# A two-layer decoder trunk: maxima over partitions taken by GpSimd, and a reordered first layer

## The chip, the cores and the metric

The kernel runs on one core of one Trainium2 chip. The metric is the time of one execution on the device in microseconds (us); before the change the median of two runs is 1400.21 us (1398.36 to 1402.06). Engines are named as in the profile: PE (matmul) with PEld (its weight loads), DVE (VectorE), ACT (ScalarE), POOL (GpSimd) and SP (which issues the DMAs here).

## The reference

One sequence of 1024 tokens with 1024 channels in float32 goes through two layers. Each layer projects x to [main | memory query | main gate | memory gate], computes a main branch and a cross-attention into 256 memory tokens (4 heads of 128), gates both with silu, projects back and normalizes:

```python
h = x @ w_in
y_main = main_fn(h[..., :D_MAIN])
y_mem = memory_attention(q_mem, mem, w_mem_kv)
y = concat([y_main * silu(g_main), y_mem * silu(g_mem)])
x = layer_norm(ALPHA * x + y @ w_out, ln_g, ln_b)
```

In layer 0 the main branch is a causal pooling: four groups of 256 channels, trailing means over 2, 4, 8 and 16 tokens minus the token, then a 256x256 map per group and a scale per channel. In layer 1 it is causal attention of 16 heads with forget gates. The change touches layer 0 alone.

## The kernel before, in words

Everything stands transposed: channels on the 128 partitions, tokens along the free axis. A float32 product is made of three products of parts. There are two ways to cut a number.

*Plain parts* (`hi_lo`, lines 168-173): `hi` is the float32r copy (ACT, L171), `lo` the remainder in bf16 (DVE, L172) and `top` a bf16 copy of the number (ACT, L173, or POOL, L166, where a caller passes `gp_copy`). `three` (L162) pairs them: hi with hi, top with lo, lo with top. `split_w` loads a weight piece of 128x512 on SP and cuts it.

*Scaled halves* (`halves_of`, L253-255): a number times a power of two as an f16 value (ACT, L254) and its f16 remainder (DVE, L255). This needs a scale that holds for the whole tensor, so a maximum over all partitions: `bound` (L234-245) reduces on DVE (L238), writes 128 numbers to DRAM (SP, L239), reads all of them back into each partition (SP, L241), reduces again (DVE, L242) and rounds to a power of two (L243, L244). `scale_of` inverts it (L249, L250).

`slab_pair` (L257-321) computes two column slabs of x @ w_in (two times 128 channels by 1024 tokens) in seven steps of 12 products, 84 in all, in place of 96, by Strassen's scheme in Winograd's form. It loads four weight blocks, takes their absolute sums (ACT, L266), calls `bound`, forms four differences of blocks on POOL (L273), and then for each step cuts one block or difference with `halves_of` and multiplies it with one of seven combinations of x (`XC`). The evacuations (L279, L287, L299) undo the scale. The first subtraction writes the tile into which the absolute values of L266 are thrown, so it waits for them.

Layer 0 runs in this order:

1. x is loaded in eight tiles and cut in plain parts (`load_x`, L626-632); two slabs of pooling group 0 are computed plainly (`slab`, L698-702). ACT sums absolute values of x (L706), and `bound` is called for x (L707).
2. Memory keys and values are projected, four heads each (`mem_kv`, L328-369, products of L347). After each head but the first, `combine` (L719-725) cuts one of the seven combinations of x in halves: 28 splits of 128x512 on ACT and DVE. In between POOL forms 16 differences and sums of blocks of x in place (L725).
3. `pooled(0)` forms the pooled values of group 0. Two `slab_pair`s make the four memory queries, cut again in plain parts; one makes the gates of group 0; `pool_out` (L666-681) multiplies the pooled values with their map.
4. Memory attention, with two `slab_pair`s of gates pumped in between.
5. For groups 1, 2, 3: a pair of inputs, `pooled`, a pair of gates, `pool_out`, and some weights of the output projection (`out_proj.split`). Then the output projection.

So `bound` is called twelve times: once for x and once in each of eleven pairs. PE's order is written out by hand (`manual_schedule`); the other engines' orders are planned by the framework from the program's order and when operands come. Each engine runs its instructions in its order, and SP its DMAs: a DMA that waits holds those behind it. Weight blocks land in a ring of six `raw` tiles, the cut ones in a ring of eight `w` tiles.

Of the kernel before, what the change touches and what calls it, by code (L numbers as in the profile page):

```python
# [18 lines left out]
P = 128  # L19
# [53 lines left out]
def trunk_kernel(ctx, tc, x, xT, memT, win, wk, wv0, wv, wmk, wmv, wout, poolw, pscale, lng, lnb, bforget, out):  # L73
# [74 lines left out]
    class Split:  # L148
# [5 lines left out]
        def __getitem__(self, at):  # L154
            part = Split.__new__(Split)
            part.hi, part.lo, part.top = self.hi[at], self.lo[at], self.top[at]
            return part

# [9 lines left out]
    def hi_lo(to, src, pinned=False, top=None):  # L168

        pin = tc.keep_in_program_order if pinned else lambda ins: ins  # L170
        pin(nc.scalar.copy(to.hi, src))  # L171
        pin(nc.vector.tensor_tensor(to.lo, src, to.hi.bitcast(F32), ALU.subtract))  # L172
        (top or nc.scalar.copy)(to.top, src)  # L173
# [6 lines left out]
    def split_w(src_dram, shape):  # L180
        r = raw(shape)
        nc.sync.dma_start(r, src_dram)
        to = parts_of(wt, shape)
        (gp_hi_lo if low[0] else hi_lo)(to, r)
        return to
# [48 lines left out]
    def bound(sums):  # L234

        m, e = tiny(1), tiny(1)
        d = dram.tile([P, 1], F32, name=nm("bound"))
        nc.vector.tensor_reduce(m, sums, AX.X, ALU.max)  # L238
        nc.sync.dma_start(d, m)  # L239
        every = sb([P, P], "every", 2, F32, more[0])  # L240
        nc.sync.dma_start(every, d.rearrange("p o -> (p o)").partition_broadcast(P))  # L241
        nc.vector.tensor_reduce(m, every, AX.X, ALU.max)  # L242
        nc.vector.tensor_scalar(m, m, 2.0 ** -100, None, ALU.max)  # L243
        nc.vector.tensor_scalar(e.bitcast(I32), m.bitcast(I32), 0x7F800000, None, ALU.bitwise_and)  # L244
        return e
# [10 lines left out]

    def slab_pair(one, two, XC, dest, done):  # L257
# [3 lines left out]
        sums = tiny(4)  # L261
        for b, src in zip(bs, (one[0], two[0], two[1], one[1])):
            nc.sync.dma_start(b, src)
        for j, b in enumerate(bs):
            junk = ts[0].rearrange("p a b -> p (a b)").bitcast(BF16)[:, :NH].rearrange("p (a b) -> p a b", a=4)
            nc.scalar.activation(junk, b, AF.Abs, accum_out=sums[:, j : j + 1])  # L266
        e = bound(sums)
        sc = scale_of(e, "wsc")
        un = sb([P, 1], "wun", 3, F32, more[0])
        nc.vector.tensor_tensor(un, e, xun, ALU.mult)  # L270
# [57 lines left out]
    def mem_kv(l):  # L328

        ms = [parts_of(T, [P, 4, NMEM]) for _ in range(2)]  # L330
# [6 lines left out]
        def project(w_dram):  # L337

            acc = ps([P, NH], "pj", 2)[:, :NMEM]
            ws = [split_w(w_dram[pc], [P, 4, P]) for pc in range(2)]  # L340
            parts = (1, 2, 0) if len(projected) % 2 else (0, 1, 2)
            projected.append(acc)
            for i in parts:
                for pc in range(2):
                    w, m = three(ws[pc], ms[pc])[i]
                    for k in range(4):
                        nc.tensor.matmul(  # L347
                            acc, w[:, k, :], m[:, k, :],
                            start=(i, pc, k) == (parts[0], 0, 0), stop=(i, pc, k) == (parts[2], 1, 3),
                        )  # L350
                        if k % 3 == 0:
                            spread()
            return acc
# [259 lines left out]
    X = parts_of(stream, [P, KT, S])  # L613
# [5 lines left out]
    with tc.tile_pool(name="in0", bufs=1) as in0:  # L619
# [6 lines left out]
        def load_x(kt, parts=1):  # L626
            r = bt(dt=F32)
            for i in range(parts):
                cols = slice(i * S // parts, (i + 1) * S // parts)
                nc.sync.dma_start(r[:, cols], xT[kt, :, cols])  # L630
                hi_lo(X[:, kt, cols], r[:, cols], top=gp_copy)
            xs.append(r)

        first = [[split_w(win[0, 0, 0], [P, 4, P])], []]
        load_x(0, 2)
        first[1].append(split_w(win[0, 1, 0], [P, 4, P]))
        for kt in range(1, 4):
            load_x(kt)
        for f in range(2):
            first[f].append(split_w(win[0, f, 1], [P, 4, P]))  # L640
# [76 lines left out]
        changes = {0: ((b21, b21, b22, ALU.add), (b11, b21, b11, ALU.subtract)), 3: ((b21, b22, b11, ALU.subtract),), 2: ((b12, b12, b11, ALU.subtract),)}  # L717

        def combine(k):  # L719
            src = (b11, b11, b12, b21, b21, b12, b22)[k]  # L720
            for kt in range(4):
                halves_of(XC[0][k][:, :, kt, :], src[kt], xsc)
            for to, a, b, op in changes.get(k, ()):
                for kt in range(4):
                    nc.gpsimd.tensor_tensor(to[kt], a[kt], b[kt], op)  # L725

        with tc.manual_schedule(engines={PE}):
            kv = mem_kv(0)
            for h in range(2 * MH):
                kv[1 + h // MH](h % MH)  # L730
                if h:
                    combine(h - 1)
            pms = pooled(0, us)
            qs = [parts_of(bt, [P, S]) for _ in range(MH)]
# [452 lines left out]
```

## Time and profile before

| | us |
|---|---|
| median of two runs | 1400.21 |
| the profiled execution | 1397.46 |
| its span, first to last instruction | 1395.8 |
| PE busy in the span | 1202.3 |
| DVE, ACT, POOL busy | 908.1, 758.4, 337.1 |

The mean granted clock of the tensor engine is 0.932. The profile shows one execution. A page lists busy times, the span in 40 slices, DMA queues and the costliest groups of instructions. Other views give busy time by stretch, waits (who waited for whom, in total, how often, the longest), and a timeline (start, duration, engine, line, operation, output<-input, and in brackets the idle time before it and what ended it). A line can be that of a helper: L172 is every remainder of plain parts.

### The profile page before, as it was taken

To read this page: it belongs to the slowest core of one execution; us is meant where nothing else is said; L and a number is where in the kernel's file an instruction comes from. 1 tells how busy PE (TensorE), PEld (TensorE's weight loads), DVE (VectorE), ACT (ScalarE), POOL (GpSimd) and SP (SyncE) were. 2 spreads that over 40 slices of the span, in tenths; PEclk is the share of its full clock that TensorE was granted. 3 is DMA by queue.
4 is the path that set the end of the run, shared out by engine and by line. 5 is a ranking of instruction groups with operands and counts; after the bars stand their busy time and mean duration, and the time that the engine had idled before them with its cause. 6 is when DMAs were issued, how large, how long until landed. Compare 5 with 4: busy or idle time off the path is not lost. (4 is left out here: it accounts for less than half of the span.)

```text
span 1395.8 us, 20190 instructions
## 1 busy us (share of the span) xinstructions
PE 1202.3 (86%) x6886; PEld 726.7 (52%) x6886; DVE 908.1 (65%) x2033; ACT 758.4 (54%) x1605; POOL 337.1 (24%) x429
## 2 busy tenths in 40 slices
PE   8635857557776689998999999999999999999997
PEld 4422323333332245556667766666666666665554
DVE  7774536566665754557357457888788788876564
ACT  7674425445443462336577336777677677767220
POOL 6431110112332300000000004434443453462000
PEclk9777988788998889999999999999999999999999
DMA  6343332344332262334244447799698698998331
GB/s 199 90 80 54 47 52 56 65 113 85 70 77 55 78 218 76 106 113 145 69 110 112 126 113 166 162 197 189 150 201 198 154 193 191 222 225 261 133 130 61
DMA packets 270871, 179.48 MB, mean 129 GB/s; under 512 B 214192, under 2 KB 229168, under 8 KB 270768
## 3 DMA queue, kind: packets, MB, share of 16 engines
q1 hardware_dynamic: 270768, 178.19, 52.7%
q8 instruction: 54, 0.88, 0.3%
q14 instruction: 49, 0.40, 0.1%
HBM read 95.76 MB, written 22.62 MB: 85 GB/s over the span
## 5 line engine op out<-in xcount | busy, mean ns | idle before, releaser
L223 PE MATMUL pj<-A,w 128*128 128x512 bf16 (+1 forms) x1872 | 448.6, 391 | 5.3 <-ACT A L171 2.4
L314 PE MATMUL pj<-A,w 128*128 128x512 f16 x696 | 172.8, 410 | 87.8 <-ACT w L254 36.2
L223 PEld LDWEIGHTS <-w 128*128 128x128 bf16 x1264 | 114.0, 98 | 140.6 <-issue 19.4
L314 PEld LDWEIGHTS <-w 128*128 128x128 f16 x696 | 72.3, 104 | 184.6 <-issue 78.6
L978 DVE SCALAR_TENSOR_TENSOR P<-T,s,P 128x512 f16<-128x512 f32 x192 | 111.5, 613 | 34.8 <-ACT P L977 33.5
L956 ACT ACTIVATE T<-MK,s 128x512 f32<-128x512 f32 x192 | 111.3, 580 | 41.6 <-DVE s L948 23.4
L223 PEld LDWEIGHTS pj<-A,w 128*128 128x128 f32 x624 | 115.2, 190 | 31.0 <-ACT A L171 4.6
L977 ACT ACTIVATE P<-T,s 128x512 f16<-128x512 f32 x192 | 102.7, 576 | 45.9 <-ACT T L956 20.7
L542 PEld LDWEIGHTS <-T 128*128 128x128 bf16 x736 | 70.9, 98 | 88.5 <-issue 6.4
L200 PE MATMUL L<-B,B 128*128 128x512 f32 (+3 forms) x384 | 106.4, 382 | 2.7 <-DVE s L948 2.5
L314 PE MATMUL pj<-A,wx 128*128 128x512 f16 x228 | 54.3, 394 | 46.4 <-ACT wx L254 43.0
L940 POOL TENSOR_SCALAR_AFFINE_SELECT R<-R 128x128 f32<-128x128 f32 x128 | 41.0, 326 | 175.2 <-DVE s L948 129.1
L200 PEld LDWEIGHTS L<-B,B 128*128 128x128 f32 x384 | 70.6, 189 | 24.1 <-DVE s L948 6.1
L166 POOL TENSOR_SCALAR w<-raw 128x512 fp32r<-128x512 f32 x108 | 67.1, 627 | 65.0 <-PE pj L223 59.7
L948 DVE CUSTOM_DVE_ANT_0 MK<-L,R 128x512 f32<-128x512 f32 (+3 forms) x128 | 72.5, 566 | 9.1 <-PE L L200 3.6
L177 POOL TENSOR_TENSOR w<-raw,w 128x512 bf16<-128x512 f32 x54 | 69.5, 1286 | 18.7 <-PE pj L223 16.2
L347 PE MATMUL pj<-T,w 128*128 128x256 bf16 (+1 forms) x336 | 51.5, 307 | 23.5 <-ACT w L173 6.9
L853 POOL MEMSET G<- 128x128 f32 x1 | 0.2, 205 | 293.4 <-DVE V L484 293.4
L172 DVE TENSOR_TENSOR T<-T,T 128x1024 bf16<-128x1024 f32 x23 | 28.1, 1223 | 58.4 <-ACT T L171 36.4
L172 DVE TENSOR_TENSOR w<-raw,w 128x512 bf16<-128x512 f32 x55 | 42.0, 764 | 32.1 <-PE pj L223 14.8
L314 PEld LDWEIGHTS <-wx 128*128 128x128 f16 x228 | 22.8, 101 | 75.6 <-ACT wx L254 43.8
L1000 PE MATMUL O<-T,V 128*64 128x128 f16 (+1 forms) x1152 | 57.6, 221 | 2.7 <-DMA T<-P 2.6
(323 smaller groups left out, 2290.7 us busy)
## 6 DMA issues: line engine op xcount, KB each, us to landing
raw<-in_win_dram SPq DMA_DIRECT2D x80, 256.0 KB, 2.8
raw<-in_wout_dram SPq DMA_DIRECT2D x33, 256.0 KB, 3.1
B<-B SPq DMA_DIRECT2D x32, 256.0 KB, 4.1
R<-cumd SPq DMA_DIRECT2D x16, 512.0 KB, 4.9
y0d<-Y SPq DMA_DIRECT2D x12, 512.0 KB, 2.7
T<-y0d SPq DMA_DIRECT2D x12, 512.0 KB, 3.6
T<-y1d SPq DMA_DIRECT2D x11, 512.0 KB, 5.2
rawx<-in_win_dram SPq DMA_DIRECT2D x16, 256.0 KB, 2.6
```

The source lines that it names most:

```text
L166: nc.gpsimd.tensor_scalar(to, src, 1.0, 1.0, ALU.mult, ALU.mult)
L172: pin(nc.vector.tensor_tensor(to.lo, src, to.hi.bitcast(F32), ALU.subtract))
L177: nc.gpsimd.tensor_tensor(to.lo, src, to.hi.bitcast(F32), ALU.subtract)
L200: nc.tensor.matmul(acc, a, b, start=i == 0, stop=i == len(terms) - 1)
L223: nc.tensor.matmul(accs[n], a[:, k, :], b[:, pc * 4 + k, n * NH : (n + 1) * NH], start=seen[n] == 1, stop=seen[n] == 3 * KT,)
L314: nc.tensor.matmul(bank[name], w[:, e0, kt, :], xc[:, e1, kt, :], start=bool(opens) and i == kt == 0, stop=k in (2, 5, 6) and i == 2 and k ...
L542: nc.tensor.matmul(accs[a][nh], y, w, start=kt == 8 and i == 0, stop=kt == 7 and i == 2,)
L948: nc.vector.tensor_tensor_reduce(p[:, lo:up], lg, R[:, lo:up], 1.0, top, ALU.add, ALU.min, m[:, n : n + 1])
L956: nc.scalar.activation(e, p[:, lo:up], AF.Exp, bias=top, scale=-1.0, accum_out=sums[:, n, hd % 2, i : i + 1],)
L977: nc.scalar.activation(pair[:, lo:up], e, AF.Copy, scale=r)
L978: nc.vector.scalar_tensor_tensor(pair[:, L + lo : L + up], e, r, pair[:, lo:up], ALU.mult, ALU.subtract)
L1000: nc.tensor.matmul(acc[rows, (i % 4) * P : (i % 4) * P + P], v[:, b, 2 * j : 2 * j + (1 if e else 2), :].rearrange("p e d -> p (e d)"), pt ...
```

## The change

- `bound` no longer goes through DRAM: between DVE's first reduction and the rounding stands one GpSimd instruction, an all-reduce (max) of one number over 128 partitions. Two DMAs, one DVE reduction and a 128x128 tile go.
- A class `Same` has `top` equal to `hi`, and its `lo` is float32r. x, the first four weight pieces of the first two slabs, the memory and its weights in layer 0 are cut so: the third copy goes, and the two smaller products are float32r products.
- The first two memory queries are computed by a new `two_slabs`: the same scaled halves, but four weight blocks with four blocks of x in 96 products, with no differences. It evacuates into plain parts at once.
- `combine` becomes `combos`: four blocks of x are cut first (two beside the value heads 0 and 1, two after the memory), 8 block splits in all in place of 7; POOL's 16 operations on x and the last four splits come after `two_slabs` in the program. `pooled(0)` moves behind the second query pair.
- Groups go in the order 3, 2, 1, and the `pool_out` of a group comes after the next group's pair of inputs.

```diff
     def bound(sums):
-        m, e = tiny(1), tiny(1)
-        d = dram.tile([P, 1], F32, name=nm("bound"))
+        m, every, e = tiny(1), tiny(1), tiny(1)
         nc.vector.tensor_reduce(m, sums, AX.X, ALU.max)
-        nc.sync.dma_start(d, m)
-        every = sb([P, P], "every", 2, F32, more[0])
-        nc.sync.dma_start(every, d.rearrange("p o -> (p o)").partition_broadcast(P))
-        nc.vector.tensor_reduce(m, every, AX.X, ALU.max)
-        nc.vector.tensor_scalar(m, m, 2.0 ** -100, None, ALU.max)
+        nc.gpsimd.partition_all_reduce(every, m, P, bass_isa.ReduceOp.max)
+        nc.vector.tensor_scalar(m, every, 2.0 ** -100, None, ALU.max)
...
+    class Same(Split):
+        def __init__(self, hi, lo):
+            self.hi = self.top = hi
+            self.lo = lo
...
-        (top or nc.scalar.copy)(to.top, src)
+        if not isinstance(to, Same):
+            (top or nc.scalar.copy)(to.top, src)
...
+    def two_slabs(one, two, xh, xun, junk, evac):
+        bs = [[raw([P, 4, P]) for _ in range(2)] for _ in range(2)]
+        for p in range(2):
+            for j, src in enumerate((one, two)):
+                nc.sync.dma_start(bs[p][j], src[p])
+        sc, un = pair_scale(bs[0] + bs[1], junk, xun)
+        ws, accs = {}, {}
+        for half in range(2):
+            for p in range(2):
+                for j in range(2):
+                    if half == 0:
+                        ws[p, j] = wt([P, 2, 4, P], F16)
+                        halves_of(ws[p, j], bs[p][j], sc)
+                    if p == 0:
+                        accs[half, j] = ps([P, NH], *(("pj", 2) if half == 0 else ("L", 3)))
+                    acc = accs[half, j]
+                    for i, (e0, e1) in enumerate(((0, 0), (0, 1), (1, 0))):
+                        for kt in range(4):
+                            nc.tensor.matmul(acc, ws[p, j][:, e0, kt, :], xh[half][p][e1][:, kt, :],
+                                start=p == i == kt == 0, stop=p == 1 and i == 2 and kt == 3)
+                    if p == 1:
+                        evac(j, slice(half * NH, (half + 1) * NH), acc, un)
...
-        ms = [parts_of(T, [P, 4, NMEM]) for _ in range(2)]
+        make = parts_of if l else same_of
+        ms = [make(T, [P, 4, NMEM]) for _ in range(2)]
...
-    X = parts_of(stream, [P, KT, S])
+    X = same_of(stream, [P, KT, S])
...
+        def combos(k):
+            if k == 0:
+                direct(b11, xh[0][0])
+            if k == 1:
+                direct(b12, xh[0][1])
+            if k == 2:
+                direct(b21, extra)
+            if k == 3:
+                direct(b22, xh[1][1])
+            if k == 4:
+                change(b21, b21, b22, ALU.add)
+                change(b11, b21, b11, ALU.subtract)
+                direct(b11, [XC[0][1][:, e] for e in range(2)])
+            if k == 5:
+                direct(b21, [XC[0][3][:, e] for e in range(2)])
+                change(b12, b12, b11, ALU.subtract)
+                change(b21, b22, b11, ALU.subtract)
+            if k == 6:
+                direct(b21, [XC[0][4][:, e] for e in range(2)])
+                direct(b12, [XC[0][5][:, e] for e in range(2)])
...
                 kv[1 + h // MH](h % MH)
-                if h:
-                    combine(h - 1)
-            pms = pooled(0, us)
+                if h in (4, 5):
+                    combos(h - 4)
             qs = [parts_of(bt, [P, S]) for _ in range(MH)]
-            for h in (0, 2):
-                wide = [G() for _ in range(2)]
-                run(plain_pair(8 + h, wide, lambda j, cols, t: hi_lo(qs[h + j][:, cols], wide[j][:, cols])))
+            combos(2)
+            combos(3)
+            two_slabs(win[0, 8], win[0, 9], xh, xun, ..., q_evac)
+            for k in (4, 5, 6):
+                combos(k)
+            wide = [G() for _ in range(2)]
+            run(plain_pair(10, wide, lambda j, cols, t: hi_lo(qs[2 + j][:, cols], wide[j][:, cols])))
+            pms = pooled(0, us)
...
-            for g in range(1, 4):
+            late = None
+            for k, g in enumerate((3, 2, 1)):
                 us = [u_tile() for _ in range(2)]
                 run(plain_pair(2 * g, us))
+                if late:
+                    pool_out(*late)
                 pms = pooled(g, us)
                 ys = [y_tile() for _ in range(2)]
                 run(gate_pair(12 + 2 * g, ys))
-                pool_out(g, pms, ys)
-                out_proj.split((4, 8, 8)[g - 1])
+                late = g, pms, ys
+                out_proj.split((4, 8, 8)[k])
+            pool_out(*late)
```

`direct` cuts a block of x in halves in four splits of 128x512 (ACT and DVE), `change` is four POOL operations of 128x512, and `pair_scale` holds the absolute sums, `bound` and the scale that stood in `slab_pair`.

More of the change, by code (lines that the diff above doesn't have):

```diff
@@ L4 @@
 import concourse.bass as bass
+import concourse.bass_isa as bass_isa
 import concourse.tile as tile
@@ L255, in halves_of, with pair_scale @@
         nc.vector.scalar_tensor_tensor(to[:, 1], src, sc, to[:, 0], ALU.mult, ALU.subtract)
+    def pair_scale(bs, junk, xun):
+        sums = tiny(len(bs))
+        for j, b in enumerate(bs):
+            nc.scalar.activation(junk, b, AF.Abs, accum_out=sums[:, j : j + 1])
+        e = bound(sums)
+        un = sb([P, 1], "wun", 3, F32, more[0])
+        nc.vector.tensor_tensor(un, e, xun, ALU.mult)
+        return scale_of(e, "wsc"), un
+    def two_slabs(one, two, xh, xun, junk, evac):
[16 more added lines that the diff above has]
+                        for kt in range(4):
+                            nc.tensor.matmul(
+                                acc, ws[p, j][:, e0, kt, :], xh[half][p][e1][:, kt, :],
+                                start=p == i == kt == 0, stop=p == 1 and i == 2 and kt == 3,
+                            )
+                    if p == 1:
+                        evac(j, slice(half * NH, (half + 1) * NH), acc, un)
     def slab_pair(one, two, XC, dest, done):
@@ L260, in slab_pair @@
         b11, b12, b22, b21 = bs = [raw([P, 4, P]) for _ in range(4)]
-        sums = tiny(4)
         for b, src in zip(bs, (one[0], two[0], two[1], one[1])):
             nc.sync.dma_start(b, src)
[L264 to L270, printed above, removed]
+        sc, un = pair_scale(
+            bs, ts[0].rearrange("p a b -> p (a b)").bitcast(BF16)[:, :NH].rearrange("p (a b) -> p a b", a=4), xun,
+        )
         t1, t2, t3, t4 = ts
@@ L339, in project @@
             acc = ps([P, NH], "pj", 2)[:, :NMEM]
-            ws = [split_w(w_dram[pc], [P, 4, P]) for pc in range(2)]
+            ws = [split_w(w_dram[pc], [P, 4, P], make) for pc in range(2)]
             parts = (1, 2, 0) if len(projected) % 2 else (0, 1, 2)
@@ L639, in trunk_kernel @@
         for f in range(2):
-            first[f].append(split_w(win[0, f, 1], [P, 4, P]))
+            first[f].append(split_w(win[0, f, 1], [P, 4, P], same_of))
         for kt in range(4, KT):
```

40 lines of the change are left out of this document (26 added, 14 removed).

## The prediction

> **What bounds the kernel now.** I read the page first (engines, slices), then busy time by stage, then the waits of the tensor engine, of VectorE and of the DMA queue SP, then the timeline of one bound.
>
> ```profile
> PE 1202.3 (86%) x6886; PEld 726.7 (52%) x6886; DVE 908.1 (65%) x2033; ACT 758.4 (54%) x1605; POOL 337.1 (24%) x429
> PE   8635857557776689998999999999999999999997
> ```
> ```profile
> 0.00:36.00 36.00, 29.80 (x106) 14.32 (x106) 25.29 (x42) 28.13 (x47) 22.03 (x19) 0.91 0.62 193
> 36.00:91.00 55.00, 34.24 (x192) 24.97 (x192) 45.34 (x76) 37.51 (x71) 23.02 (x15) 0.75 0.31 91
> 91.00:114.00 23.00, 0.34 (x3) 0.13 (x2) 6.55 (x21) 8.31 (x16) 3.78 (x3) 0.57 0.45 48
> 114.00:152.00 38.00, 32.50 (x132) 13.81 (x131) 19.21 (x32) 19.40 (x40) 11.30 (x8) 0.86 0.47 57
> 152.00:192.00 40.00, 33.14 (x147) 15.00 (x144) 20.74 (x34) 14.66 (x24) 1.27 (x1) 0.91 0.11 37
> 192.00:313.00 121.00, 62.72 (x458) 38.86 (x456) 65.40 (x146) 53.04 (x148) 14.66 (x11) 0.77 0.40 77
> 313.00:418.00 105.00, 82.08 (x336) 35.19 (x337) 68.39 (x106) 51.87 (x98) 32.85 (x22) 0.87 0.41 81
> 418.00:502.00 84.00, 58.57 (x242) 25.74 (x241) 58.32 (x88) 38.05 (x65) 21.93 (x17) 0.86 0.26 70
> 502.00:1396.00 894.00, 868.87 (x5282) 558.73 (x5280) 598.89 (x1494) 507.44 (x1103) 206.24 (x334) 0.99 0.62 156
> ```
>
> The columns are the stretch, its length, busy time of PE, PEld, DVE, ACT and POOL, the granted clock, the DMA share and GB/s. From 502 us on PE is busy 869 of 894 us, and the change touches none of that. Layer 0, the first 502 us, holds PE for 333 us: 169 us are idle, at a clock of 0.57 to 0.91. The waits of PE in that part say where:
>
> ```profile
> PE pj L314 <- ACT wx L254: 43.0, 2, 22.5
> PE pj L314 <- ACT w L254: 36.2, 2, 22.7
> PE pj L314 <- DVE e L279: 22.0, 7, 6.0
> PE pj L314 <- DVE s L243: 9.8, 1, 9.8
> PE pj L314 <- ACT P L299: 8.6, 1, 8.6
> PE pj L314 <- DVE s L244: 7.3, 1, 7.3
> PE pj L314 <- ACT G L299: 6.9, 1, 6.9
> PE pj L347 <- DVE s L243: 5.8, 1, 5.8
> PE L L200 <- DVE Y L680: 5.7, 1, 5.7
> ```
> ```profile
> DVE s L242 <- DMA every<-bound: 81.3, 11, 13.4
> ```
> ```profile
> SPq L241 <- DMA bound<-s: 79.8, 12, 7.8
> ```
>
> Each wait is us in total, times, longest. L254 cuts weights with a scale that waits for `bound`; L243, L244, L279, L299 and L680 stand behind L242 on VectorE or wait for the same scale. Twelve times a maximum goes to DRAM and comes back: VectorE is held at L242 for 81.3 us in all, SP at L241 for 79.8 us with the weight loads behind it. One of them in order of time:
>
> ```profile
> 93.25 1.04 ACT L171 CAST T<-G 128x1024 fp32r<-128x1024 f32 x1
> ...
> 95.14 0.63 ACT L266 ACTIVATE A<-raw 128x512 bf16<-128x512 f32 x1
> ...
> 98.42 0.16 DVE L238 TENSOR_REDUCE s<-s 128x1 f32<-128x4 f32 x1 [1.63 <-ACT A L266]
> 98.46 1.26 POOL L273 TENSOR_TENSOR A<-raw,raw 128x512 f32<-128x512 f32 x1 [10.83 <-ACT A L266]
> 98.63 0.56 SPq L239 DMA_DIRECT2D bound<-s  x1
> ...
> 99.80 2.60 POOL L273 TENSOR_TENSOR A<-raw,A 128x512 f32<-128x512 f32 x2
> ...
> 111.92 0.29 DVE L242 TENSOR_REDUCE s<-every 128x1 f32<-128x128 f32 x1 [13.35 <-DMA every<-bound]
> ...
> 113.79 15.27 PE L314 MATMUL pj<-A,w 128*128 128x512 f16 x60 [22.66 <-ACT w L254]
> ```
>
> The round trip is 111.92 - 98.63 = 13.3 us, and the scale adds 1.9 until the first product. The three Pool subtractions that the second product needs (L273) are over long before.
>
> **The change, part by part.** Durations are of the profiled execution, 1397.5 us for a span of 1395.8; the median of the runs, 1400.2, is 2.7 above it, and I add that at the end.
>
> *The bounds.* Two DMA issues and a wait leave SP, one 0.29 us reduction leaves VectorE, twelve reductions over partitions enter GpSimd. VectorE's next instruction (the max with 2^-100) now waits for POOL instead of a DMA; behind it stand the same evacuations, and PE behind those. No row shows that reduction. Below, it is bounded by a POOL copy of one column; above, nothing bounds it but the trip that it replaces is the first mark.
>
> ```profile
> 343.36 0.65 POOL L656 COPY G<-P 128x1 f32<-128x1 f32 x1
> ```
> ```profile
> DMA to landing us min/median/max: 3.3/6.0/9.4
> ```
>
> So 0.65 us at one end and 13.3 or more at the other. I take the nearer kind of row: something that must collect a value from 128 partitions, the outward leg of the old trip, 6.0 us to its landing. In POOL's queue the subtraction of 98.46 starts as VectorE's reduction ends, and the next two follow without a gap, so up to three of 1.3 stand before the new instruction: 6.0 + 3.9 = 9.9 us from sums to maximum, 3.4 less than 13.3. Some of that goes back: the subtractions left behind it now end after the maximum, where they had ended 9 us before it. I take 3.0 a bound. The nine waits of PE above sum to 145 us; without the first pair's 22.7 and the 5.8 of the memory stage, 117 us stand behind the ten other pair bounds, 11.7 each, so 3.0 can come out in full: -30. The bound of x is in the memory stage below. By the bounds: a maximum in 2 us would give about -9 each, one in 20 us +7 each.
>
> [...]
>
> *First slabs and memory as float32r pairs.* Gone are the third part's copies: 9 on POOL (x) and 24 on ACT (4 + 16 weight pieces, 4 memory pieces).
>
> ```profile
> L166 POOL TENSOR_SCALAR A<-B 128x1024 bf16<-128x1024 f32 (+1 forms) x9 | 14.1, 1574 | 5.7 <-DMA B<-in_xT_dram 5.7
> ```
> ```profile
> L255 DVE SCALAR_TENSOR_TENSOR A<-B,xsc,A 128x512 f16<-128x512 f32 x28 | 26.1, 963 | 0.7 <-ACT A L254 0.4
> L725 POOL TENSOR_TENSOR B<-B,B 128x512 f32<-128x512 f32 x12 | 20.9, 1758 | 7.7 <-DVE A L255 7.7
> L254 ACT ACTIVATE A<-B,xsc 128x512 f16<-128x512 f32 x28 | 18.6, 715 | 0.0
> L173 ACT CAST w<-raw 128x512 bf16<-128x512 f32 x11 | 6.8, 620 | 0.0
> L725 POOL TENSOR_TENSOR B<-B 128x512 f32<-128x512 f32 x4 | 6.3, 1594 | 12.5 <-DVE A L255 12.5
> ```
> ```profile
> L223 PE MATMUL pj<-A,w 128*128 128x512 bf16 x415 | 100.0, 381 | 0.0
> L223 PE MATMUL pj<-A,w 128*128 128x512 f32 x202 | 54.6, 404 | 0.0
> ```
>
> That is 14.1 us of POOL and 24 x 0.62 = 14.9 of ACT. On PE 64 slab products turn from bf16 to f32, by the last rows (of 1000 to 1200 us) 23 ns more each: +1.5. In the first 36 us PE is busy 29.8, so little is to be had: -2 after that cost (from +2 to -5).
>
> *Memory stage (36 to 91 us).* PE needs 34.2 of 55; VectorE is busy 45.3, ACT 37.5. Twenty casts leave ACT (12.4). Of the 28 splits of x (26.1 on VectorE, 18.6 on ACT) only 8 stay at the values' heads, 24 follow (one block of x is split twice as often, 32 in all). VectorE falls to about 45.3 - 20 x 0.96 = 26, ACT to 37.5 - 12.4 - 20 x 0.72 = 11, and PE's 34 plus 3 (128 products at 23 ns more) becomes the limit. The 5.8 us behind x's bound shrink too. Floor 37, ceiling 55; I take 43, as the loads and each head's evacuation still break PE's stream: -12.
>
> *First query pair plain.* The casts of the pooled values that kept ACT until 95.14 come later in the program (4 us), and this pair has no subtractions before its reduction (13.3 - 6.0 = 7.3): -11. It has 96 products instead of 84, at 15.27/60 = 0.25 us: +3. The 16 differences of x (20.9 + 6.3 = 27 us of POOL) lay under the memory stage; now they, and 16 splits, must end under these 96 products (24 us), with the second pair's reduction and subtractions in the same queue. I count 27 + 5 + 6 - 24, less the 12 of the 48 products that stand before the first that needs the last of them: +2 of a new wait. Together -6 (from -15 to +12).
>
> *Pooling products a pair later.* One wait of 5.7 us (L200 behind L680) is nearly all a VectorE held by L242, already counted; the pooled values get a pair's time, over 30 us. -2.
>
> Sum: -30 - 2 - 12 - 6 - 2 = -52; 1397.5 - 52 = 1345.5, and with the 2.7 to the median 1348.
>
> **The rivals.** *Cheap reduction:* POOL answers in about 4 us from sums to maximum, as a queue with a 0.65 us copy allows. Then ten bounds and the first give 6 more each: 1348 - 65 = 1283. For it: POOL had been idle for 10.8 us before 98.46, so nothing need stand ahead of the reduction. Against: all 128 partitions must meet.
>
> *Gain given back in POOL:* reduction and subtractions do not follow each other freely, so the maximum comes early but the second product's operand late, and the pair starts as late as before. Then -30 becomes about 0 and the differences of x cost some 4 more: 1382. For it: second products now depend on work behind the reduction. [...]
>
> *Slower:* the reduction holds POOL's queue so long that VectorE waits longer at L243 than at L242 now. All else gives -22, so from 13.3 + 2.2 = 15.5 us on the kernel is slower, and from 18.3 by 2%. At 20 us: 10 x 10.1 more than forecast, 1449. For it: nothing above bounds the price, and three trips of it would stand in line before the second query pair. Against: the trip already pays two landings in DRAM.
>
> **How the numbers follow.** My forecast 0.40 (own range 1325 to 1374), cheap 0.20 (1260 to 1325), given back 0.18 (1370 to 1405), slower 0.22 (1405 to 1490). Faster by over 2% (about what a measurement can tell from no change) is below 1372: 0.38 + 0.20 + 0.02 = 0.60. Slower is above 1428: 0.19 of the last case. The rest, 0.21, is the same. Half of the cheap case lies below 1285 and half of the slow one above 1432: those are the ends.
>
> **What would show it.** Right: the wait of VectorE's max for POOL near 7 to 10 us, 13 before; SP no longer stopped; the memory stage about 43 us; layer 0 over near 450 us. Wrong: a wait above 13 us there (slower); the first product early and the second waiting for L273's successors (given back); the second query pair's second and fifth steps waiting for x's differences longer than 5 us; a memory stage still of 55 us, which would mean that its loads set it.

## The result, and the profile after

The changed kernel takes 1346.27 us (median of two runs, 1342.56 to 1349.98) beside 1400.21: a ratio of 0.9615 with a 95% interval of 0.9488 to 0.9741. A later run of the same two kernels with more executions (e7 below), the one that the experiments are set against, gave 1346.17 beside 1409.43, a ratio of 0.9544 (0.9521 to 0.9568). The forecast was 1348.0 in a range of 1285 to 1432. The profiled execution after takes 1342.56 us for a span of 1340.8; its mean granted clock is 0.955, it was 0.932.

Engines and PE's slices from the page of the changed kernel, then its busy time by stage (the columns are those of the prediction's tables; the bounds stand where each stage's last or first product stands now):

```profile
PE 1195.3 (89%) x6826; PEld 734.4 (55%) x6898; DVE 901.9 (67%) x2017; ACT 746.5 (56%) x1580; POOL 323.0 (24%) x428
PE   8668764876878899989999999999999999999997
```
```profile
0.00:32.50 32.50, 28.65 (x105) 20.19 (x106) 20.52 (x48) 28.01 (x45) 2.12 (x8) 0.95 0.71 257
32.50:71.00 38.50, 27.81 (x193) 26.55 (x192) 37.14 (x55) 25.82 (x53) 19.90 (x13) 0.87 0.29 98
71.00:83.90 12.90, 0.02 (x1) 0.02 (x2) 11.16 (x28) 7.58 (x15) 5.48 (x5) 0.64 0.18 41
83.90:157.60 73.70, 66.46 (x288) 29.16 (x289) 40.06 (x66) 34.15 (x59) 15.35 (x13) 0.95 0.16 51
157.60:270.10 112.50, 66.70 (x459) 39.90 (x458) 65.19 (x144) 53.52 (x148) 12.86 (x12) 0.81 0.29 82
270.10:445.60 175.50, 141.63 (x573) 59.73 (x577) 128.55 (x187) 89.95 (x161) 61.19 (x45) 0.92 0.25 82
445.60:1341.00 895.40, 864.09 (x5215) 558.82 (x5281) 599.29 (x1494) 507.45 (x1103) 206.09 (x334) 0.99 0.62 155
```

Set against the lengths of the same stages before (the prediction's rows, with 38 and 40 taken together, and 105 and 84):

| stage | before | after | difference |
|---|---|---|---|
| first slabs | 36.0 | 32.5 | -3.5 |
| memory | 55.0 | 38.5 | -16.5 |
| wait for the first query product | 23.0 | 12.9 | -10.1 |
| queries, gates of group 0, its pooling products | 78.0 | 73.7 | -4.3 |
| memory attention with two pairs of gates | 121.0 | 112.5 | -8.5 |
| groups | 189.0 | 175.5 | -13.5 |
| the rest | 894.0 | 895.4 | +1.4 |

All of the gain is in layer 0, which ends at 445.6 us in place of 502. The waits of PE, VectorE and SP in the first 450 us of the changed kernel (total, times, longest, in us):

```profile
PE pj L352 <- ACT w L261: 61.4, 10, 17.1
PE pj L293 <- ACT w L261: 12.9, 1, 12.9
PE pj L352 <- DVE e L317: 10.9, 6, 4.0
PE pj L352 <- DVE w L262: 9.9, 6, 2.9
PE pj L386 <- ACT MK L184: 7.8, 3, 4.7
```
```profile
DVE s L250 <- POOL s L249: 21.0, 9, 8.2
```
```profile
SPq L305 <- DVE w L262: 90.1, 19, 13.3
```

In the changed kernel's numbering L249 is the all-reduce and L250 the max behind it, L311 the subtractions of a pair, L352 a pair's products, L293 those of `two_slabs`, L261 and L262 the halves of weights, L317 an evacuation, L386 the memory's products, L763 and L767 the splits and differences of x. VectorE's stop at the bound fell from 81.3 us to 21.0, and SP's at it is gone: what SP waits longest for now is a weight tile that VectorE has yet to read. But PE still waits 61.4 us for scaled weights (L261), so the bound is cheaper and not cheap. One bound in order of time, on VectorE, POOL and PE (start, duration, instruction, in brackets the idle time before it):

```profile
166.51 0.16 DVE L248 TENSOR_REDUCE s<-s 128x1 f32<-128x4 f32 x1 [1.64 <-ACT A L268]
166.56 1.26 POOL L311 TENSOR_TENSOR A<-raw,raw 128x512 f32<-128x512 f32 x1 [26.38 <-ACT A L268]
...
174.45 0.38 POOL L249 PARTITION_ALL_REDUCE s<-s  x1 [6.63 <-issue]
174.86 0.15 DVE L250 TENSOR_SCALAR s<-s 128x1 f32<-128x1 f32 x1 [8.19 <-POOL s L249]
...
176.47 1.89 PE L352 MATMUL pj<-A,w 128*128 128x512 f16 x4 [17.15 <-ACT w L261]
```

From the sums (166.51) to the maximum (174.86) it takes 8.35 us; over the eleven bounds of weights it is 4.8 to 10.7 us, where it had been 12.0 to 13.5 before. The reduction itself is 0.38 us of that. One subtraction, 1.26 us, slips ahead of it, and then POOL stands for 6.63 us with "issue" as the reason: it waits for nothing that the profile shows. POOL's own timeline shows the same pause on the way back:

```profile
166.56 1.26 POOL L311 TENSOR_TENSOR A<-raw,raw 128x512 f32<-128x512 f32 x1 [26.38 <-ACT A L268]
174.45 0.38 POOL L249 PARTITION_ALL_REDUCE s<-s  x1 [6.63 <-issue]
181.54 1.25 POOL L311 TENSOR_TENSOR A<-raw,A 128x512 f32<-128x512 f32 x1 [6.71 <-issue]
182.87 1.27 POOL L311 TENSOR_TENSOR A<-rawx,A 128x512 f32<-128x512 f32 x1
```

So POOL loses 6.63 us here when it goes from a subtraction to a reduction and 6.71 on the way back, and 0.08 between two subtractions. The view of line L249 shows what marks these places:

```profile
L249 POOLq MODIFY_POOL_CONFIG  x24: 3/11/13, 1.6 to 403.4; - x24
L249 POOL PARTITION_ALL_REDUCE s<-s x12: 376/377/385, 24.2 to 409.9; - x12
```

An instruction of POOL's sequencer, MODIFY_POOL_CONFIG, of some 11 ns, carries the reductions' line 24 times. The subtractions' line (L311) has 22 more, of 82 to 83 ns, and that of x's differences (L767) two of 83, and always two stand together: 24 changes from one kind of work to the other, twelve into a reduction and twelve out of it. In POOL's timeline a pause of 5.7 to 7.2 us stands at each, but for the first, which falls into a longer idle time. So each return to the other kind of work pays again. What POOL does in the pause, the trace does not show.

### The profile page after: what moved, and what is told of

The parts are those of the page before. It is cut to its first block, busy times and chain, and to the rows that moved or that the text cites. A ratio compares the mean times of both kernels' runs of the same rounds, so it can differ in the third digit from the quotient of the medians.

```text
span 1340.8 us, 20096 instructions
## 1 busy us (share of the span) xinstructions
PE 1195.3 (89%) x6826; PEld 734.4 (55%) x6898; DVE 901.9 (67%) x2017; ACT 746.5 (56%) x1580; POOL 323.0 (24%) x428
## 3 DMA queue, kind: packets, MB, share of 16 engines
HBM read 94.97 MB, written 22.61 MB: 88 GB/s over the span
## 5 line engine op out<-in xcount | busy, mean ns | idle before, releaser
L234 PE MATMUL pj<-A,w 128*128 128x512 bf16 (+1 forms) x1827 | 441.7, 390 | 7.6 <-ACT A L181 2.2
L352 PE MATMUL pj<-A,w 128*128 128x512 f16 x624 | 159.0, 414 | 78.5 <-ACT w L261 61.4
L234 PEld LDWEIGHTS <-w 128*128 128x128 bf16 x1216 | 109.4, 98 | 131.6 <-issue 14.4
L352 PEld LDWEIGHTS <-w 128*128 128x128 f16 x624 | 63.9, 105 | 169.6 <-ACT w L261 67.0
L234 PEld LDWEIGHTS pj<-A,w 128*128 128x128 f32 x656 | 120.9, 189 | 32.8 <-ACT A L181 4.7
L1057 ACT ACTIVATE P<-T,s 128x512 f16<-128x512 f32 x192 | 102.9, 576 | 47.3 <-ACT T L1036 20.7
L182 DVE TENSOR_TENSOR T<-T,T 128x1024 bf16<-128x1024 f32 x23 | 28.1, 1223 | 55.7 <-ACT T L181 29.0
L386 PE MATMUL pj<-T,w 128*128 128x256 f32 (+1 forms) x336 | 48.0, 300 | 14.5 <-ACT MK L184 7.8
L182 DVE TENSOR_TENSOR w<-raw,w 128x512 bf16<-128x512 f32 (+1 forms) x54 | 40.9, 758 | 26.7 <-PE pj L234 14.9
L1080 PEld LDWEIGHTS <-V 128*64 128x64 f16 (+1 forms) x1152 | 50.2, 104 | 14.4 <-issue 5.9
L352 PE MATMUL pj<-A,wx 128*128 128x512 f16 x216 | 51.5, 395 | 6.8 <-DVE e L317 6.8
```

The source lines that it names most:

```text
L234: nc.tensor.matmul(accs[n], a[:, k, :], b[:, pc * 4 + k, n * NH : (n + 1) * NH], start=seen[n] == 1, stop=seen[n] == 3 * KT,)
L352: nc.tensor.matmul(bank[name], w[:, e0, kt, :], xc[:, e1, kt, :], start=bool(opens) and i == kt == 0, stop=k in (2, 5, 6) and i == 2 and k ...
L1057: nc.scalar.activation(pair[:, lo:up], e, AF.Copy, scale=r)
L1080: nc.tensor.matmul(acc[rows, (i % 4) * P : (i % 4) * P + P], v[:, b, 2 * j : 2 * j + (1 if e else 2), :].rearrange("p e d -> p (e d)"), pt ...
```

## The experiments

Each ratio is to the kernel before on the same chip, with its 95% interval. A gain in us is worked out from these ratios and 1408 us; single executions of one kernel and the unchanged part behind layer 0 (887 to 902 us in these profiles) vary by several us. Twelve kernels ran in three groups; the time of the kernel before in them was 1407.62, 1409.43 and 1407.98 us. The theory at the start (A): the gain is the sum of three separate parts, cheaper bounds, fewer copies of the first inputs, and plain first queries, and the bound's own price is POOL's change between two kinds of work. The first rival: nearly all of the gain comes from one part alone. The second: the reduction is slow in itself, or waits for the subtraction ahead of it.

**The reduction alone, put into the kernel before** (e1):

```diff
-        nc.sync.dma_start(d, m)
-        every = sb([P, P], "every", 2, F32, more[0])
-        nc.sync.dma_start(every, d.rearrange("p o -> (p o)").partition_broadcast(P))
-        nc.vector.tensor_reduce(m, every, AX.X, ALU.max)
-        nc.vector.tensor_scalar(m, m, 2.0 ** -100, None, ALU.max)
+        nc.gpsimd.partition_all_reduce(every, m, P, bass_isa.ReduceOp.max)
+        nc.vector.tensor_scalar(m, every, 2.0 ** -100, None, ALU.max)
```

> The kernel before with one edit: the maximum over partitions by GpSimd. Theory A (the reduction pays by itself: 0.4 us of work with a gap of some 6.5 us ahead of it, so about 8 us from sums to maximum where the DRAM trip took 13.3): ten exposed bounds give 3 to 5 us each and x's bound 6, so 1355 to 1370. Theory B (the gaps around the reduction eat the gain, and the rest of the change made it): 1390 to 1405.

Measured 1366.85 us, ratio 0.972 (0.9687 to 0.9753): 39 us less than before, as theory A said.

**The changed kernel with the bound through DRAM again** (e2, the same lines the other way):

> The changed kernel with the maximum again through DRAM. Theory A: each bound is some 5 us longer, ten of them with an idle tensor engine behind, x's and the first pair's on top: 1380 to 1395. Theory B: 1341 to 1355, since nothing is lost with the reduction.

Measured 1387.6 us, ratio 0.9863 (0.9829 to 0.9896): all else in the change gives 1.4%, 19 us. Against the whole change (0.9544) the reduction is worth 0.0319 of 1408, 45 us, here; alone it was 39. VectorE's wait is the old one again, and the memory stage and the wait behind it are 6.9 and 7.0 us longer than in the changed kernel:

```profile
DVE s L253 <- DMA every<-bound: 94.8, 11, 13.9
```
```profile
32.50:77.90 45.40, 29.48 (x193) 28.51 (x191) 38.25 (x65) 29.73 (x59) 19.93 (x13) 0.81 0.37 114
77.90:97.80 19.90, 0.04 (x1) 0.00 (x0) 12.57 (x27) 7.63 (x15) 6.64 (x4) 0.60 0.25 30
```

The reduction is the larger part, but not the only one.

**Pooling products at once again** (e3):

```diff
-            for k, g in enumerate((3, 2, 1)):
+            for k, g in enumerate((1, 2, 3)):
                 us = [u_tile() for _ in range(2)]
                 run(plain_pair(2 * g, us))
-                if late:
-                    pool_out(*late)
                 pms = pooled(g, us)
...
-                late = g, pms, ys
+                pool_out(g, pms, ys)
```

> The changed kernel with the pooling products of a group again right behind its gates, groups 1, 2, 3. Theory A (the two that wait were VectorE's, held by the bound): 1344 to 1352. Rival (GpSimd's sums for the windows now stand behind the gaps around the reductions, and only the late products hide that): 1356 to 1375, with the tensor engine waiting at the pooling products.

Measured 1341.49 us, ratio 0.9539 (0.9503 to 0.9575), and the change itself 0.9544 (0.9521 to 0.9568): no difference. The late products and the new order of the groups gain nothing on the whole. In the profiled run the output projection begins at 451.8 us, 3 to 6 later than in the two profiles of the changed kernel (445.6, and 448.6 in e7), and what follows is 8 to 9 shorter; why is left open.

**Three parts again for x, the first slabs and the memory** (e4):

```diff
-        make = parts_of if l else same_of
+        make = parts_of
...
-    X = same_of(stream, [P, KT, S])
+    X = parts_of(stream, [P, KT, S])
...
-                hi_lo(X[:, kt, cols], r[:, cols])
+                hi_lo(X[:, kt, cols], r[:, cols], top=gp_copy)
...
-            first[f].append(split_w(win[0, f, 1], [P, 4, P], same_of))
+            first[f].append(split_w(win[0, f, 1], [P, 4, P]))
```

> The changed kernel with x, the first slabs' weights and the memory cut in three parts again (bf16 copies by ACT, for x by GpSimd). Theory A: the copies set the pace of the memory stage and part of the start: 3 us at the start and 8 to 12 in the memory stage come back, 1355 to 1362. Rival (the memory stage is shorter because SP and VectorE no longer stand at x's bound, and the copies ran beside other work): 1344 to 1351.

Measured 1357.61 us, ratio 0.9649 (0.9617 to 0.9682): cutting in two parts is worth 0.0105 of 1408, 15 us. But it shows up elsewhere than expected. These rows are the stretch from the first to the last memory product and the wait behind it, and PE's two longest waits in the first 450 us of this kernel:

```profile
32.90:60.40 27.50, 23.16 (x192) 20.10 (x192) 22.47 (x48) 27.50 (x56) 1.56 (x1) 1.00 0.56 169
60.40:88.60 28.20, 0.04 (x2) 0.02 (x2) 23.09 (x36) 14.95 (x31) 18.84 (x13) 0.57 0.08 19
```
```profile
PE pj L352 <- ACT w L261: 76.7, 13, 17.0
PE pj L293 <- ACT w L261: 28.2, 1, 28.2
```

ACT is busy through the whole 27.5 us of the memory products, and the work on x is put off behind them: POOL is busy 18.84 us in the wait and not 19.90 beside the products. So the memory ends at 60.4 us, before the changed kernel's 71.0, and the first query product comes at 88.6, after its 83.9. Only 4.7 us of the 15 are there, and at the start there is next to nothing: the first memory product comes at 32.9 us, in the changed kernel at 32.55. The others lie in later pairs, whose code this edit does not touch: L352 waits for ACT 13 times in place of 10, 76.7 us in place of 61.4. The framework plans the other engines' orders anew for each program, and what that gives there was not taken apart.

**The changed kernel itself** (e7), in the group of the next three:

> The changed kernel itself, to stand beside the others on one chip. All theories: 0.95 to 0.965 of the kernel before. Against it e3_not_late (0.954 of the kernel before) shows whether the late pooling products are worth anything.

Measured 1346.17 us, ratio 0.9544 (0.9521 to 0.9568).

**The subtractions of every pair on VectorE** (e5), so that POOL keeps its reductions and the window sums:

```diff
-            nc.gpsimd.tensor_tensor(to, a, b, ALU.subtract)
+            nc.vector.tensor_tensor(to, a, b, ALU.subtract)
```

> The changed kernel with the four subtractions of each pair on VectorE. Theory A (the gaps of 6.2 to 7.2 us on GpSimd around each reduction belong to changing between two kinds of work, the reduction itself takes 0.4 us): where one reduction follows another on GpSimd the gap is gone and the maximum comes within 1 us of the sums; some seven exposed bounds give 5 to 7 us each, 11 x 4 x 0.7 us more on VectorE take back 5 to 15: 1300 to 1325. Rival (the gap is the reduction's own time, in front of what the profile marks): the maximum still comes 7 us after the sums, and the time is 1340 to 1360.

Measured 1280.14 us, ratio 0.9069 (0.9036 to 0.9102): 66 us less than the changed kernel, and 20 less than I expected at best. The same bound in this kernel:

```profile
157.76 0.16 DVE L248 TENSOR_REDUCE s<-s 128x1 f32<-128x4 f32 x1 [1.63 <-ACT A L268]
157.83 0.68 DVE L311 TENSOR_TENSOR A<-raw,raw 128x512 f32<-128x512 f32 x1
158.13 0.63 POOL L249 PARTITION_ALL_REDUCE s<-s  x1 [30.68 <-DVE s L248]
...
158.79 0.15 DVE L250 TENSOR_SCALAR s<-s 128x1 f32<-128x1 f32 x1 [0.28 <-POOL s L249]
...
161.41 1.03 PE L352 MATMUL pj<-A,w 128*128 128x512 f16 x2 [10.84 <-ACT w L261]
```

Sums to maximum now take 158.79 - 157.76 = 1.03 us, 8.35 in the changed kernel. A subtraction costs VectorE 0.68 us where it cost POOL 1.26. The second rival falls: the reduction answers in 0.63 us here, behind 30.68 us in which POOL was idle, and in 0.63 to 0.64 us at the next three bounds, where POOL comes from a reduction. PE's waits for L261 in this kernel:

```profile
PE pj L352 <- ACT w L261: 20.1, 2, 10.8
```

**The subtractions held behind the reduction on POOL** (e6):

```diff
-        nc.gpsimd.partition_all_reduce(every, m, P, bass_isa.ReduceOp.max)
+        reduced[0] = nc.gpsimd.partition_all_reduce(every, m, P, bass_isa.ReduceOp.max).ins
...
-            nc.gpsimd.tensor_tensor(to, a, b, ALU.subtract)
+            with tc.issue_after(reduced[0]):
+                nc.gpsimd.tensor_tensor(to, a, b, ALU.subtract)
```

> The changed kernel with each pair's reduction ahead of its subtractions in GpSimd's order. Theory A: the change ahead of the reduction runs while GpSimd is idle, the maximum comes within 1 us of the sums, 7 earlier; the change behind it then stands before all four subtractions, so the second product comes some 11 us after the first instead of being ready 8 after: 2 to 5 us a pair, 1310 to 1335. Rival (own time): no gain, and subtractions later: 1350 to 1380.

Measured 1316.97 us, ratio 0.9337 (0.9309 to 0.9365): as theory A said, 29 us less than the changed kernel, less than half of what e5 gained. The same bound, VectorE, POOL and PE:

```profile
161.61 0.16 DVE L250 TENSOR_REDUCE s<-s 128x1 f32<-128x4 f32 x1 [1.63 <-ACT A L270]
161.91 0.38 POOL L251 PARTITION_ALL_REDUCE s<-s  x1 [30.62 <-DVE s L250]
162.32 0.15 DVE L252 TENSOR_SCALAR s<-s 128x1 f32<-128x1 f32 x1 [0.55 <-POOL s L251]
...
163.93 4.71 PE L355 MATMUL pj<-A,w 128*128 128x512 f16 x12 [9.51 <-ACT w L263]
...
169.59 2.48 POOL L314 TENSOR_TENSOR A<-raw,raw 128x512 f32<-128x512 f32 x2 [7.30 <-ACT e L328]
...
174.55 1.89 PE L355 MATMUL pj<-A,w 128*128 128x512 f16 x4 [5.91 <-ACT w L263]
```

The maximum comes 0.71 us after the sums: POOL had been idle for 30.62 us ahead of the reduction, and no pause stands between the sums and its start (0.30 us). The subtractions pay on the way back: they start 7.30 us after the reduction (put down to ACT here, to "issue" with 6.71 to 7.13 us at three other bounds), and the second step's products wait another 5.91 us. This is the prediction's rival of the gain given back in POOL, seen in part.

**A pair for the first queries again** (e8):

```diff
-            two_slabs(win[0, 8], win[0, 9], xh, xun, ..., q_evac)
             for k in (4, 5, 6):
                 combos(k)
-            wide = [G() for _ in range(2)]
-            run(plain_pair(10, wide, lambda j, cols, t: hi_lo(qs[2 + j][:, cols], wide[j][:, cols])))
+            for h in (0, 2):
+                wide = [G() for _ in range(2)]
+                run(plain_pair(8 + h, wide, lambda j, cols, t: hi_lo(qs[h + j][:, cols], wide[j][:, cols])))
```

> The changed kernel with the first two memory queries by a pair of 84 products again, after all the combinations of x. Theory A (plain queries let the products start before the differences of x and need no subtractions): the first product 8 to 15 us later and 3 us fewer products: 1350 to 1362. Rival (the planner has the differences done by then anyway, since GpSimd ran them under the memory stage): 1340 to 1350.

Measured 1357.07 us, ratio 0.9628 (0.9598 to 0.9659): the plain queries are worth 0.0084 of 1408, 12 us. The first products of its PE timeline:

```profile
91.09 18.40 PE L352 MATMUL pj<-A,w 128*128 128x512 f16 x72 [20.16 <-ACT w L261]
```

The first query product comes at 91.09 us, 7.2 later than in the changed kernel (83.9), a little less than expected. The output projection begins 5.6 later (451.2 us, 445.6 there; 2.6 against e7's profile). The other half of the 12 us stands behind that, in code that the edit does not touch, and no view shows a reason for it; so some 3 to 6 us are shown for the plain queries.

**Subtractions on VectorE and pooling products at once** (e9, the edits of e3 and e5 together):

> Subtractions on VectorE as in e5_subs_dve (0.907 of the kernel before) and pooling products right behind the gates, groups 1, 2, 3. If the late products are worth nothing by themselves, as e3_not_late against e7_changed_again says: within 5 us of e5, 1275 to 1286. Rival (with short bounds the tensor engine catches up with the window sums, and the late products hide them): 1288 to 1305.

Measured 1280.87 us, ratio 0.9086 (0.906 to 0.9112): as e5. With cheap bounds too the late products bring nothing on the whole.

**Window sums on VectorE as well** (e10), so that behind the differences of x POOL has reductions alone in layer 0:

```diff
-            for u, eng in zip(us, (nc.vector, nc.gpsimd)):
+            for u, eng in zip(us, (nc.vector, nc.vector)):
```

> e5_subs_dve with the window sums of both pooling tiles on VectorE, so that GpSimd changes between its two kinds of work only around the differences of x. Theory A: five more reductions come within 1 us of their sums, 2 to 5 us each where the tensor engine stands behind them; VectorE gets some 22 us of sums: 1270 to 1282. Rival (VectorE is the limit in the groups' stage by now): 1284 to 1300.

Measured 1269.38 us, ratio 0.9009 (0.8983 to 0.9035). The view of the reduction's line shows four marks where the changed kernel had 24 (with the two at x's differences three changes in layer 0), and the longest waits of PE in the first 450 us are these:

```profile
L249 POOL PARTITION_ALL_REDUCE s<-s x12: 377/641/1777, 23.8 to 331.4; - x12
L249 POOLq EVENT_SEMAPHORE  x10: 17/17/17, 89.0 to 331.3; - x10
L249 POOLq MODIFY_POOL_CONFIG  x4: 8/10/11, 1.5 to 76.1; - x4
```
```profile
PE pj L352 <- ACT w L261: 23.9, 3, 10.8
PE pj L293 <- ACT w L261: 12.8, 1, 12.8
PE pj L386 <- ACT MK L184: 7.7, 3, 4.7
```

The 23.9 us stand in place of 61.4, but e5 had 20.1 there already: the 8 us beyond e5 (ratios 0.9069 and 0.9009) come from elsewhere. In e5's profile two maxima among the last groups still come 7.55 and 4.02 us after their sums, behind window sums on POOL (with pauses of 5.81 and 6.26 us ahead of the reductions). In e10's the latest comes after 5.54 us, and there VectorE is busy with other work (the reduction starts 0.32 us after the sums). Which wait of PE this ends was not taken apart.

**The control: subtractions on VectorE with the bound through DRAM** (e11, the edits of e2 and e5):

> Control for e5_subs_dve: the changed kernel with the maximum through DRAM and the subtractions on VectorE. Theory A (they gain only because GpSimd then does not change its work around a reduction): 1383 to 1400, as e2_dram_bound or slower by VectorE's extra work. Rival (subtractions on VectorE are faster whatever the bound): 1330 to 1360.

Measured 1381.12 us, ratio 0.9808 (0.9781 to 0.9834), beside 0.9863 for e2: 0.55%, 8 us, and the intervals touch. With the reduction on POOL the same edit was worth 66 us. So the faster subtraction does not make e5's gain by itself; it takes the reduction on POOL with no subtractions beside it.

**All of it: e10 with pooling products at once** (e12):

> e10_all_dve with pooling products right behind the gates, groups 1, 2, 3. The lower of e9_dve_not_late and e10_all_dve within 5 us if the two edits do not touch each other; above both by 5 to 15 if the sums on VectorE come too late for products that follow at once.

Measured 1265.68 us, ratio 0.8993 (0.8965 to 0.9021): the fastest of all, 10% below the kernel before, with e10 within the interval. Engines from its page:

```profile
PE 1179.1 (93%) x6898; PEld 730.9 (58%) x6898; DVE 906.6 (72%) x2077; ACT 746.7 (59%) x1580; POOL 242.0 (19%) x368
```

## Why the prediction was right, step by step

*What bounds the kernel.* Right: only layer 0 moved. From the kernel before (span 1395.8, PE busy 1202.3) to the changed kernel in e7's profiled run (span 1345.0, PE busy 1203.1) PE's idle time fell by 193.5 - 141.9 = 51.6 us and its busy time not at all. The 1.5, 3 and 3 us of longer or added products that the terms had counted are not in it: in the memory stage PE is busy 27.8 us and not 37, at a granted clock of 0.87 in place of 0.75.

The experiments place the gains better than the changed kernel alone does. From their PE timelines, in us, one profiled execution each:

| kernel | first slabs | memory | wait for the first query product | from there to the output projection |
|---|---|---|---|---|
| before | 36.0 | 55.1 | 22.7 | 388.0 |
| e1, reduction alone | 36.0 | 49.8 | 16.9 | 366.7 |
| e2, all but the reduction | 32.5 | 45.4 | 19.9 | 389.1 |
| e4, three parts again | 32.9 | 27.5 | 28.2 | 374.7 |
| e8, a pair for the first queries | 33.1 | 37.9 | 20.2 | 360.1 |
| the changed kernel | 32.6 | 38.4 | 12.9 | 361.7 |

*The bounds, -30.* The size holds. The three stages behind the first query product gained 26.3 us (8.5 and 13.5, and 4.3 with the twelve more products in it), where the prediction's terms come to -30 + 3 + 2 - 2 = -27; by the last column the reduction is worth 21.3 us there put into the kernel before and 27.4 taken out of the changed one. With the 7.3 and 5.8 that it counted in other stages, the reduction should bring 43; e2 gives 45, e1 39. Of the 52 that leaves some 9 for all else; e2 has 19, so all else was put too low. The price had nearly the right sum from wrong parts, and that is luck. It was put together as 6.0 for the meeting of 128 partitions and 3.9 for three subtractions ahead, 9.9 us; the bound shown takes 8.35, of which the reduction is 0.38, one subtraction 1.26, and POOL's change between two kinds of work 6.63. The 6.0 was also misread: it is the median over both legs of the old trip. The outward leg alone, in the kernel before:

```profile
L239 SPq DMA_DIRECT2D bound<-s x12: 319/329/562, 31.1 to 444.6; - x12
DMA to landing us min/median/max: 7.2/7.9/9.4
```

With 7.9 the same sum would have given 11.8 us, and less than half of the gain. The step "something that must collect a value from 128 partitions, the outward leg of the old trip" was the wrong likeness too: a transfer to DRAM says nothing about that reduction, and the 0.65 us copy, the lower bound that the prediction left, was the nearer row (0.38, in e5 0.63).

*What POOL's changes took back.* A pause of 5.7 to 7.2 us stands on both sides of the reductions, at all of the 24 changes but the first. It does not take all of the -30 back, but a part of it. PE's waits inside the pairs, added up by step from the PE timelines (over 0.3 us at the start of a step, over 1 us within one), say where. At the first step they are 50.8 us, and 56.6 before without the first query pair. At the second and third they are 20.3, and were nothing before: there the subtractions mostly come late (2.1 us with them on VectorE, e5). At the fourth to seventh they are 13.6, and were 54.9: those stand mostly behind evacuations and VectorE, which the bound no longer holds for long (21.0 us in place of 81.3). So the gain is mostly that of a freed VectorE, as the prediction's mechanism has it, and its rival "gain given back", which would have been 1382, is true in part: the prediction let 0.4 us a bound go back, and it is about 2. The 4 us more that this rival had for the differences of x were the author's estimate, and no run shows them. With the reduction alone (e1) the second step waits 34.2 us.

*First slabs, -2:* -3.5. The copies are not shown as the cause: with them back (e4) the stage takes 32.9 us, and with the reduction alone (e1) 36.0 as before. What shortened it is open.

*Memory, -12:* -16.5. The direction is right, but the cause that the prediction gave, ACT's third copies, is not shown: with the copies back the stage is shorter still (27.5 us), as work on x moves behind it. Taken with the wait that follows, the two stages last 77.8 us before, 51.3 in the changed kernel and 55.7 with the copies, so the copies are worth some 4 of the 26 us there. The bound is worth more, 14.0 by e2 and 11.1 by e1, and the plain queries 6.8 by e8. Beyond the bound's 7 us, what shortened the memory stage itself was not separated from the new order of the splits. The step that failed is what becomes of the other engines. "VectorE falls to about 26, ACT to 11": they are busy 37.1 and 25.8 us, since 21 splits of x (L763) and nearly all of the differences (POOL busy 19.9 us) still run beside the memory products, though they come later in the program.

*First query pair, -6.* The wait ahead of it fell by 10.1 (said 11: 4 and 7.3). By e2 the bound is worth 7.0 of this wait, by e8 the plain queries 7.3; the two overlap. The new wait of 2 for x's differences did not come: they ran under the memory, not under the 96 products, and PE has no gap at the second pair's first products. e8 gives 12 us for this part in the whole time, with the twelve more products inside, and 3 to 6 of them in layer 0.

*Late products, -2:* 0, by e3 and by e9.

*The sum.* By the experiments the parts are 45 + 15 + 12 + 0 = 72 where the whole is 0.0456 of 1408, 64. Each of the three is a difference of two ratios with some 5 us of uncertainty, so this neither shows that the parts overlap nor that they are separate. That the forecast, 1348.0, lies within 2 us of the first result is luck in part: by the later ratio the gain is 64 us where 52 were forecast.

*The rivals.* "Cheap reduction" gave 1283 for an answer in 4 us; the reduction is as cheap as that and cheaper, but in the pairs of the changed kernel it always stands behind a change of POOL's work. e5 removes most of these, and runs in 1280.14; that the two times are so near is luck, since e5's maximum mostly comes 1.0 us after the sums and part of its gain is shorter products, as said next. "Slower" had the reduction at 15.5 us and more: no bound here comes near.

One gain lies outside any term of the prediction. From e7 to e5 the span falls by 68.1 us (1345.0 to 1276.9): 47.3 of it is less idle time of PE, and 20.8 less busy time for the same 6898 products, at a mean granted clock of 0.970 in place of 0.952. Between the first query product and the output projection the clock is 0.94 in place of 0.87, and a product of the pairs takes 387 ns in place of 412. The prediction counted waits alone, and so did the expectation of e5. It is no rule that closing gaps shortens products: from the kernel before to e7 51.6 us of gaps closed, the clock in that stretch rose only from 0.84 to 0.87, and a product of the pairs took 406 and 412 ns. What sets the clock there is not shown.

## What to carry to other kernels

Here an instruction on POOL had two prices: its own time (0.38 us), and that of changing over from what stood there before it (5.7 to 7.2 us). Read the second in the idle time before it (put down to "issue" at 15 of the 24 changes, to an engine at the others), and count the alternations, not the instructions. Where one operation on POOL sits on the path and its neighbours there are of another kind, move the neighbours away: that gave 66 us here, about as much as the whole change's 64. And experiments of one part each, with a control for the cure, tell what a sum that comes out right hides.

## What the runs showed of the hardware

- A reduction of one number over 128 partitions with its result in all of them takes 0.38 to 0.39 us on POOL in the changed kernel, where all twelve stand behind other work, and mostly 0.63 to 0.64 (up to 1.78) behind another reduction (e5, e10). The way through DRAM took 13.3 us in the kernel before (98.63 to 111.92).
- In the changed kernel each change of POOL between that reduction and elementwise work comes with a pause of 5.7 to 7.2 us, in both directions, at 23 of 24 changes; the first falls into 22.61 us of idle time. In e10's layer 0 there are three changes. Where POOL was idle for 30.62 us ahead of the reduction (e6), the reduction started 0.30 us after the sums, with no pause on the path.
- The same 128x512 subtraction takes 1.26 us on POOL (the changed kernel) and 0.68 on VectorE (e5).
